# Subtractions from split operands joined in PSUM, and eight modulation slabs loaded ahead of the first x tiles, in a hybrid transformer block

## The chip, the cores and the metric

The kernel runs on one core of a Trainium2 chip. Time is device microseconds of one execution, lower is better. The kernel before took 1477.26, 1480.0 and 1477.43 us in three runs, median 1477.43.

## The reference

One block works on 1024 latent tokens and 256 context tokens of width 1024, in fp32. Cut to what matters here:

```python
mod = jax.nn.silu(c) @ lp['w_mod'] + lp['b_mod']      # w_mod is 1024 x 6144
sh1, sc1, g1, sh2, sc2, g2 = jnp.split(mod[:, None, :], 6, axis=-1)
h = _rms(x, lp['norm1']) * (1 + sc1) + sh1
P = _project(h, lp, rope)                              # one projection: Fourier, attention, delta rule
...
x = x + g1 * _mix_out(P, o_att, o_dn, lp['w_out'], lp['o_norm'])
x = x + g2 * _mlp(_rms(x, lp['norm2']) * (1 + sc2) + sh2, lp['w_ff1'], lp['w_ff2'])

def _mlp(h, w1, w2):
    u = jnp.maximum(h @ w1, 0.0)
    return (u * u) @ w2
```

The context tokens go through the same modulation (from c_ctx) and projection, and only feed the attention and the delta rule.

## The kernel before, in words

**Numbers in two halves.** A product in fp32 is made of three matmuls: each operand is held as a high part, rounded to the matmul's type fp32r, and a low part, the remainder. `mm3` (L238 to L241) issues high × high, high × low, low × high; so the lines L239, L240 and L241 are most of TensorE's rows. `split` (L1452 to L1454) makes the halves: ACT writes the high part (the line of the helper is L223), and an engine given by the caller subtracts it from the value to get the low part (L1454).

**Engines and queues.** V is VectorE (DVE in the profile), G is GpSimd (POOL), T is TensorE (PE), SC is ScalarE (ACT), Y is SyncE (SP), whose queue issues nearly all loads. A scheduler decides the order of each engine's instructions from the order of the code and priorities (`tc.high_priority`); where `ypin` or `pinned` is set, loads (`yd`, L231) or matmuls (`pe`, L229) keep the order of the code. Each engine works through its own queue in order.

**The start.** w_mod is read in slabs of 128 × 1024 (512 KB), eight slabs for each sixth of the modulation (a "pass", q). `mod_steps` (L314) loads one slab and issues four matmuls on it for each of its steps. Slabs live in a ring of eight buffers, later nine (L340, L406). The order of the code is: pass 0 interleaved with the transposes of the first two x tiles (L403 to L414), the columns of the modulation, pass 1 (L417), then the first projections. `load_x` (L361) loads x tiles, `rms_rows` (L354) squares and sums a tile on ACT and takes the power on POOL (L357, L358), `norm_in` (L367) scales it on DVE (L370). The rope tables are prepared on POOL at L389 to L398. The passes 4, 2 and 5 come later, as small tasks between other matmuls, from a ring of two slabs; their loads stand on SP's queue among writes to and reads from DRAM scratch (lsc, L710 and L723; tsc, L733; qd, L770).

**The MLP's operands.** The MLP multiplies by blocks, with seven products in place of eight, for which sums and differences of blocks are needed. The modulated h of the second norm is held transposed, in blocks of eight pieces of 128 × 512. `h2_first` makes the first half's blocks, named "11" and "21", as high and low parts in the dictionary HB. `h2_second` (L1539) makes the other operands:

- t1[k] = transposed second half, piece k, less block 11's piece k
- t2[k] = piece k + 4 (called 22) less t1[k]; 22[k] is that piece itself
- t3[k] = t2[k] less block 11's piece k; t4[k] = t2[k] less block 21's piece k

Only the parts of 11 and 21 exist, so a subtraction of one takes two steps: the high part (`sub` on G, or on V for k = 0), then the low part (on V), all at L1540. `h2_T` (L1446) transposes one piece: four transposes on PE (L244) into a bank of PSUM, then ACT scales it out to SBUF. Its banks come from the ring `tr2`, which holds three of the eight banks at that point: bk[0], bk[1], bk[3] (L1498).

`h2_second` is issued at high priority (L1618). Around it `ff1` (L1565) makes the products for the first two column blocks j = 0, 1: "11" and "12" first, then s1 (which uses t1), s2 (t2), s4 (22), s3 (t3) and 22 (t4), each evicted from PSUM by ACT or DVE (L1583 to L1613). `w1_prep` (L1481) makes the weights' side: sums on POOL (L1487), high parts on ACT, low parts on DVE (L1454). `gate_bc` (L1348) spreads a row of the modulation over all partitions: two small matmuls on PE (L236) and one DVE operation (L1352). In the profile a tile is named by its pool: fbase and z2a to z2c hold fp32, rbase, z1a to z1d hold fp32r, ba and bk are PSUM banks.

Of the kernel before, what the change touches and what calls it, by code (L numbers as in the profile page):

```python
# [14 lines left out]
ALU = mybir.AluOpType  # L15
AX = mybir.AxisListType

P = 128
D = 1024
# [3 lines left out]
KT = D // P  # L23
# [171 lines left out]
def body(tc, t, out):  # L195
# [3 lines left out]
    with ctx:  # L199
# [14 lines left out]
        V, G, T, Y, SC = nc.vector, nc.gpsimd, nc.tensor, nc.sync, nc.scalar  # L214

        def buf(*shape, top=False, a=None, at=None):
            return Buf(a or Fa, (P,) + shape, top, at)

        def rbuf(*shape, a=None):
            return Buf(a or Ra, (P,) + shape)  # L220
# [4 lines left out]
        def f32(ap):  # L225
            return ap.bitcast(F32)


        def pe(i):  # L229
            return tc.keep_in_program_order(i) if pinned else i  # L230

        def yd(i):
            return tc.keep_in_program_order(i) if ypin else i

        def mm(o, l, r, start, stop):
            pe(T.matmul(o, l, r, start=start, stop=stop))  # L236
# [15 lines left out]
        C = {k: cstb[a >= 256]()[:, a % 256 if a < 256 else a - 256 : b if a < 256 else b - 256] for k, (a, b) in CST.items()}  # L252
# [21 lines left out]
        cs = csb()  # L274
# [35 lines left out]
        def mod_pass(*a):  # L310
            for _ in mod_steps(*a):
                pass

        def mod_steps(q, slabs, bank, queue=Y):  # L314
            w = t["w_mod"]
            for k in range(KT):
                sl = slabs.next()
                sl = sl if isinstance(sl, tuple) else (sl,)
                n = D // len(sl)
                for z, part in enumerate(sl):  # L320
                    yd(queue.dma_start(part, w[0, k * P : (k + 1) * P, q * D + z * n : q * D + (z + 1) * n]))
                for g in range(4):
                    mm(bank[32 * g : 32 * g + 32, 0:256], cs[:, k, :], sl[g * 256 // n][:, g * 256 % n : g * 256 % n + 256], k == 0, k == KT - 1)
                yield

        def mod_cols(bank, sets, rowbuf):
# [11 lines left out]

        rowtmp = buf(256)
        slab0 = [buf(D, a=Z2) for _ in range(8)]  # L340
        slabs = Ring([b() for b in slab0])

# [24 lines left out]
        def norm_in(xs):  # L367
            for xt in xs:
                rs = rms_rows(xt)
                V.tensor_scalar(xt, xt, rs, None, op0=ALU.mult)  # L370
# [32 lines left out]
        ypin = True  # L403
        xs0 = load_x(t["x"][0], 0, xb[0:2])
        norm_in(xs0)
        slab1 = [buf(D, a=Z2)]  # L406
        xTb = [buf(256) for _ in range(KT)]
        trb = Ring([bk[0], bk[1]])
        slabs = Ring([b() for b in slab0 + slab1])
        for k, _ in enumerate(mod_steps(0, slabs, bk[2])):  # L410
            b = trb.next()
            for q, xt in enumerate(xs0):
                tp(b[:, q * P : (q + 1) * P], xt[:, k * P : (k + 1) * P])
            act(xTb[k](), b[:, 0:256])  # L414
# [72 lines left out]
        ypin = False  # L487
# [39 lines left out]
        for p, xs in enumerate((xs1, xs2, xs3, xs4)):  # L527
            norm_in(xs)
            g, c0 = ((0, 256), (1, 0), (1, 256), (2, 0))[p]
# [104 lines left out]
        b = gb.next()  # L634
# [9 lines left out]
        b = gb.next()  # L644
# [8 lines left out]
        b = gb.next()  # L653
# [5 lines left out]
        for d in range(2):  # L659
# [32 lines left out]
        sub = Arena(Z2.base, 0)  # L692
# [56 lines left out]
        def modulations():  # L749
            (v,) = mod_rows(bk[2], 1, rowtmp())  # L750
            V.tensor_tensor(kt2(s2()), v, kt2(col[:, r_b2 : r_b2 + 8]), op=ALU.add)
            yield
            yield from mod_steps(4, mslr, bk[2])
            act(rowtmp(), bk[2][:, 0:256])
            yield
            (v,) = mod_rows(bk[2], 1, rowtmp())
            V.tensor_tensor(kt2(a2()), v, kt2(col[:, r_b2 + 8 : r_b2 + 16]), op=ALU.add)
            V.scalar_tensor_tensor(a2(), a2(), 1.0, col[:, r_n2 : r_n2 + 8], op0=ALU.add, op1=ALU.mult)
            yield
            for q, z in ((2, 0), (5, 1)):  # L760
                yield from mod_steps(q, mslr, bk[2])
                act(mrowb[z](), bk[2][:, 0:256])
                yield
# [605 lines left out]
        for n in range(NPR * 5):  # L1369
            j, k = n // 5, n % 5  # L1370
# [59 lines left out]
        rw = [[buf(4, 256) for _ in range(2)], None]  # L1430
        shr = Ring([buf(512) for _ in range(3)])
        tr2 = Ring([bk[0], bk[1]])

        def rms_ff(q):
            st = rsb[q]()
            for z in range(2):
                act(bk[2], ACC[q][:, z * 512 : z * 512 + 512], AF.Square, accum_out=st[:, z : z + 1])
            G.tensor_tensor(st[:, 0:1], st[:, 0:1], st[:, 1:2], op=ALU.add)
            G.tensor_scalar(st[:, 0:1], st[:, 0:1], 1.0 / D, EPS, op0=ALU.mult, op1=ALU.add)
            G.tensor_tensor(st[:, 1:2], st[:, 0:1], neghalf[:, 0:1], op=ALU.pow)  # L1440
# [5 lines left out]
        def h2_T(k, hf):  # L1446
            b = tr2.next()
            for q in range(4):
                tp(b[:, q * P : (q + 1) * P], ACC[q][:, k * P : (k + 1) * P])
            act(hf, b, AF.Identity, scale=a2()[:, k : k + 1], bias=s2()[:, k : k + 1])  # L1450

        def split(i, hi, lo, eng, heng=None):  # L1452
            (heng or act)(hi, i)
            eng.tensor_tensor(lo, i, f32(hi), op=ALU.subtract)  # L1454
# [37 lines left out]
        for n4 in range(4):  # L1492
# [9 lines left out]
            for q in range(NT):  # L1502
                b = omr.next()[:, 0:256]
# [26 lines left out]
        HB = {"11": [tuple(x()[:, k] for x in B11) for k in range(4)], "21": [tuple(x()[:, k] for x in B21) for k in range(4)]}  # L1530
# [6 lines left out]
        ur = Ring(slot[14:16] + slot[0:8:2] + slot[1:8:2] + slot[8:14])  # L1537

        def h2_second():  # L1539
            sub = lambda e, o, i, x: e.tensor_tensor(o, i, x, op=ALU.subtract)  # L1540
            t1, tr_ = [x() for x in slot[8:12]], Ring([x() for x in slot[12:14]])
            for k in range(4):
                h2_T(k, t1[k])
                sub(G if k > 0 else V, t1[k], t1[k], f32(HB["11"][k][0]))
                sub(V, t1[k], t1[k], f32(HB["11"][k][1]))
                split(t1[k], *HB["t1"][k], V)
            for k in range(4):
                h22 = tr_.next()
                h2_T(k + 4, h22)
                sub(V, t1[k], h22, t1[k])  # L1550
                split(t1[k], *HB["t2"][k], V)
                split(h22, *HB["22"][k], V)
            for k in range(4):
                x3 = tr_.next()
                sub(G, x3, t1[k], f32(HB["11"][k][0]))
                sub(V, x3, x3, f32(HB["11"][k][1]))
                split(x3, *HB["t3"][k], G)
                sub(G, t1[k], t1[k], f32(HB["21"][k][0]))
                sub(V, t1[k], t1[k], f32(HB["21"][k][1]))
                split(t1[k], *HB["t4"][k], V)  # L1560

        f1r = Ring(A3 + bk[2:5])
# [55 lines left out]
        with tc.high_priority(OFN3):  # L1618
            h2_second()
# [33 lines left out]
        zp2, Z2 = zone("right", Z2W, F32, "z2c")  # L1653
# [69 lines left out]
        for pn, (prods, blocks) in enumerate(PASSES):  # L1723
            for pc in range(NPC):
# [4 lines left out]
                for w in blocks:  # L1729
                    W[w] = raww.next()()  # L1730
                    j, k = int(w[0]) - 1, int(w[1]) - 1
# [7 lines left out]
                if pn == 3 and pc in (2, 3, 4, 5):  # L1739
                    q = pc - 2  # L1740
                    gated(y11[q], q, 0, lo_h)
                    gated(m3[q], q, 0, hi_h)
                for n in prods:
                    if n in WSUM:
                        x, y, op = WSUM[n]
                        V.tensor_tensor(W[x], W[x], W[y], op=op)
                        w = W[x]
                    else:
                        w = W[WRAW[n]]
# [34 lines left out]
```

## Time and profile before

| | us |
|---|---|
| three runs: median (lowest, highest) | 1477.43 (1477.26, 1480.0) |
| the profiled execution | 1475.22 |
| its span, first to last instruction | 1473.1 |
| PE busy | 1391.9 |
| DVE busy | 1026.7 |
| ACT busy | 704.6 |
| POOL busy | 657.2 |

The profiled execution is 2.2 us shorter than the median of the three runs; the span lacks 2.1 us of it. Its granted clock of TensorE is 0.972 of full speed on average. A row of the timeline gives start and length in us, engine, line, operation, the tile written and the tiles read, partitions × elements, a count, and in brackets how long the engine was idle before it and which engine and line ended that. Rows of a matmul overlap the next one: the distance of two starts is the rate. A row with "x4" stands for four instructions in a row.

### The profile page before, as it was taken

The page shows a single profiled execution, that of the slowest core. Times are in us where ns is not written, and L with a number is a line of the kernel's source. Part 1 is how long each engine was busy: PE and PEld are TensorE (multiplying, and loading weights), DVE is VectorE, ACT ScalarE, POOL GpSimd, SP SyncE. Part 2 cuts the span into 40 slices and gives each one's busy share as a digit, 9 for nine tenths or more (in the row PEclk, how much of TensorE's full clock was granted, in tenths as well). Part 3 has the DMA queues.
Part 4 walks back from the last instruction along what each step waited for, and adds up shares of the span by engine and source line. Part 5 has one row for each costly group of instructions (what it writes and reads, how often), then busy time and mean ns, then how long its engine had stood idle before and what let it go on. Part 6 is the DMA issues. An engine that isn't in the chain of part 4 may idle for free.

```text
span 1473.1 us, 28890 instructions
## 1 busy us (share of the span) xinstructions
PE 1391.9 (94%) x11438; PEld 1118.6 (76%) x11438; DVE 1026.7 (70%) x1747; ACT 704.6 (48%) x1239; POOL 657.2 (45%) x698
## 2 busy tenths in 40 slices
PE   5899888989999999989899789999999999999998
PEld 1787866766777777768799667888888888888886
DVE  0876688775878777786733898755556677676884
ACT  1743312223777777776512645554555443443331
POOL 2764653632446466465433866444343100020782
PEclk8799999989999999999999889999999999999999
DMA  9414374552001010042222214544445898776641
GB/s 327 176 58 141 95 186 122 148 109 79 9 9 25 5 36 10 10 148 72 87 82 105 92 49 143 164 152 156 158 157 185 296 395 271 249 236 210 200 158 57
DMA packets 137302, 197.65 MB, mean 134 GB/s; under 512 B 45021, under 2 KB 80463, under 8 KB 136911
## 3 DMA queue, kind: packets, MB, share of 16 engines
q1 hardware_dynamic: 136464, 195.12, 41.2%
q8 instruction: 89, 1.46, 0.4%
q10 hardware_dynamic: 703, 0.69, 0.2%
q14 instruction: 46, 0.38, 0.1%
HBM read 149.84 MB, written 45.94 MB: 133 GB/s over the span
## 4 chain that ended last, share of the span: by engine, by line
PE 46%; DVE 5%; POOL 2%; issue 1%; DMA 1%; ACT 0%; DVEq 0%; POOLq 0%; ACTq 0%; SPq 0%
PE bk L240 8%; PE bk L241 8%; PE bk L239 8%; PE ba L239 7%; PE ba L240 7%; PE ba L241 7%; DVE fbase L1540 1%; PE bk L236 1%; DVE z1c L1454 1%; DVE z1b L1321 0%; DVE rbase L984 0%; DMA fbase<-la 0%; POOL rbase L1454 0%; PE ba L236 0%; POOL z2c L1714 0%
## 5 line engine op out<-in xcount | busy, mean ns | idle before, releaser
L223 ACT ACTIVATE rbase<-fbase 128x512 fp32r<-128x512 f32 (+3 forms) x255 | 171.9, 686 | 87.6 <-PE bk L240 55.3
L223 ACT ACTIVATE fbase<-bk 128x512 f32<-128x512 f32 (+3 forms) x224 | 124.9, 561 | 150.8 <-PE bk L236 93.8
L236 PE MATMUL bk<-rbase 128*128 128x256 f32 (+1 forms) x960 | 164.5, 307 | 2.1 <-DVE rbase L984 1.1
L236 PEld LDWEIGHTS bk<-rbase 128*128 128x128 f32 (+1 forms) x960 | 127.0, 173 | 30.4 <-DVE rbase L984 1.9
L236 PE MATMUL ba<-rbase 128*65 128x512 f32 (+4 forms) x576 | 137.7, 341 | 6.3 <-DVE rbase L984 4.6
L223 ACT ACTIVATE z1c<-fbase 128x512 fp32r<-128x512 f32 (+1 forms) x120 | 76.7, 654 | 135.3 <-DMA fbase<-w_ff 49.1
L223 ACT ACTIVATE fbase<-fbase 128x512 f32<-128x512 f32 (+4 forms) x148 | 95.8, 660 | 94.5 <-POOL fbase L1606 27.2
L1487 POOL TENSOR_TENSOR fbase<-fbase 128x512 f32<-128x512 f32 x64 | 89.2, 1395 | 110.7 <-DVE z1c L1454 101.5
L1688 POOL TENSOR_TENSOR z2c<-z2c,fbase 128x512 f32<-128x512 f32 x16 | 31.8, 2010 | 203.6 <-ACT z2c L223 128.6
L960 DVE TENSOR_REDUCE fbase<-ba 128x1 f32<-128x512 f32 (+1 forms) x192 | 106.4, 594 | 19.6 <-PE ba L236 18.2
L223 ACT ACTIVATE rbase<-z1d 128x1024 fp32r<-128x1024 f32 x61 | 63.1, 1055 | 101.2 <-PE bk L240 87.3
L1454 DVE TENSOR_TENSOR z1c<-fbase,z1c 128x512 fp32r<-128x512 f32 x112 | 96.3, 866 | 19.2 <-ACT z1c L223 15.8
L1454 DVE TENSOR_TENSOR rbase<-z1d,rbase 128x1024 fp32r<-128x1024 f32 x61 | 85.5, 1416 | 31.8 <-ACT rbase L223 31.7
L984 POOL TENSOR_TENSOR rbase<-fbase,rbase 128x512 fp32r<-128x512 f32 x56 | 72.1, 1288 | 67.2 <-ACT rbase L223 63.1
L239 PE MATMUL bk<-rbase 128*128 128x512 f32 x256 | 99.6, 389 | 0.0
L240 PE MATMUL bk<-rbase 128*128 128x512 f32 x256 | 99.6, 389 | 0.0
L241 PE MATMUL bk<-rbase 128*128 128x512 f32 x256 | 99.6, 389 | 0.0
L984 DVE TENSOR_TENSOR rbase<-fbase,rbase 128x512 fp32r<-128x512 f32 x104 | 81.0, 779 | 24.6 <-ACT rbase L223 23.9
L1454 DVE TENSOR_TENSOR rbase<-fbase,rbase 128x1024 fp32r<-128x1024 f32 (+1 forms) x63 | 79.7, 1285 | 22.6 <-ACT rbase L223 22.5
L236 PEld LDWEIGHTS ba<-rbase 128*65 128x65 f32 (+1 forms) x576 | 75.7, 154 | 23.9 <-DVE rbase L984 5.7
L240 PE MATMUL ba<-rbase 128*128 128x512 f32 x192 | 74.7, 389 | 0.0
L241 PE MATMUL ba<-rbase 128*128 128x512 f32 x192 | 74.7, 389 | 0.0
(346 smaller groups left out, 3842.6 us busy)
## 6 DMA issues: line engine op xcount, KB each, us to landing
fbase<-w_ff SPq DMA_DIRECT2D x70, 512.0 KB
u<-fbase SPq DMA_DIRECT2D x112, 256.0 KB
z1d<-w_ff SPq DMA_DIRECT2D x34, 512.0 KB
z1d<-u SPq DMA_DIRECT2D x33, 512.0 KB
fbase<-w_mod SPq DMA_DIRECT2D x32, 512.0 KB
fbase<-u SPq DMA_DIRECT2D x23, 512.0 KB
z2a<-w_mod SPq DMA_DIRECT2D x16, 512.0 KB
fbase<-w_in SPq DMA_DIRECT2D x16, 512.0 KB
```

The lines of the kernel that those rows point to most:

```text
L223: return SC.activation(o, i, f, **k)
L236: pe(T.matmul(o, l, r, start=start, stop=stop))
L239: pe(T.matmul(o, lh, rh, start=start, stop=False))
L240: pe(T.matmul(o, lh, rl, start=False, stop=False))
L241: pe(T.matmul(o, ll, rh, start=False, stop=stop))
L960: V.tensor_reduce(st4[:, z : z + 1], b, AX.X, ALU.max)
L984: (G if k2 in GP and not any(a <= n < b for a, b in NGP) else V).tensor_tensor(hl[:, :, 1], p, f32(hl[:, :, 0]), op=ALU.subtract)
L1454: eng.tensor_tensor(lo, i, f32(hi), op=ALU.subtract)
L1487: G.tensor_tensor(w[nm], w[a], w[b], op=op)
L1540: sub = lambda e, o, i, x: e.tensor_tensor(o, i, x, op=ALU.subtract)
L1688: G.tensor_tensor(c, c, G2[cs_.start // 512], op=ALU.mult)
```

## The change

It has two parts.

1. The eight slabs of pass 0 are loaded as soon as the ring is made, and the ring has nine buffers from the start. These loads are pinned, so they stand on SP's queue ahead of the x tiles. `mod_steps` takes a slab that is already there from the dictionary `early`. A branch for slabs in several parts, which is no longer used, is dropped.
2. In `h2_second`, `joined(nm, k)` adds the high and the low part of a piece in PSUM: two matmuls with an identity (`idb`, copied to fp32r once) into a bank of `tr2`. One DVE subtract with that bank as an operand replaces the two subtracts. The low part of t3 is made on V, not on G.

```diff
+        early = {}
+
+        def slab_load(q, k, slabs, queue=Y):
+            sl = slabs.next()
+            yd(queue.dma_start(sl, t["w_mod"][0, k * P : (k + 1) * P, q * D : (q + 1) * D]))
+            return sl
+
         def mod_steps(q, slabs, bank, queue=Y):
...
+                sl = slab_load(q, k, slabs, queue) if (q, k) not in early else early.pop((q, k))
                 for g in range(4):
...
         slab0 = [buf(D, a=Z2) for _ in range(8)]
-        slabs = Ring([b() for b in slab0])
+        slab1 = [buf(D, a=Z2)]
+        slabs = Ring([b() for b in slab0 + slab1])
+        ypin = True
+        for k in range(KT):
+            early[0, k] = slab_load(0, k, slabs)
+        ypin = False
...
+        idb = rbuf(P)
+        V.tensor_copy(idb(), C["ident"])
...
         def h2_second():
-            sub = lambda e, o, i, x: e.tensor_tensor(o, i, x, op=ALU.subtract)
+            sub = lambda o, i, x: V.tensor_tensor(o, i, x, op=ALU.subtract)
             t1, tr_ = [x() for x in slot[8:12]], Ring([x() for x in slot[12:14]])
+
+            def joined(nm, k):
+                b = tr2.next()
+                for z in range(2):
+                    mm(b, idb(), HB[nm][k][z], z == 0, z == 1)
+                return b
+
             for k in range(4):
                 h2_T(k, t1[k])
-                sub(G if k > 0 else V, t1[k], t1[k], f32(HB["11"][k][0]))
-                sub(V, t1[k], t1[k], f32(HB["11"][k][1]))
+                sub(t1[k], t1[k], joined("11", k))
                 split(t1[k], *HB["t1"][k], V)
...
             for k in range(4):
                 x3 = tr_.next()
-                sub(G, x3, t1[k], f32(HB["11"][k][0]))
-                sub(V, x3, x3, f32(HB["11"][k][1]))
-                split(x3, *HB["t3"][k], G)
-                sub(G, t1[k], t1[k], f32(HB["21"][k][0]))
-                sub(V, t1[k], t1[k], f32(HB["21"][k][1]))
+                sub(x3, t1[k], joined("11", k))
+                split(x3, *HB["t3"][k], V)
+                sub(t1[k], t1[k], joined("21", k))
                 split(t1[k], *HB["t4"][k], V)
```

The order of instructions differs from the start to about 215 us, and in the stage of `h2_second`; the rest is the same. PE has 24 matmuls more. POOL has 15 operations fewer (eleven subtracts and four low halves). DVE has one subtract fewer, four low halves and one small copy more. Line numbers after are those of the changed kernel: L318 is the slab's load, L371 the x tile's, L1547 the subtract, L1461 the low half, L236 on rbase 128x512 a join's matmul.

At the start SP's queue read, before:

```order
L364 DMA fbase<-x 128x1024 x2
L321 DMA z2a<-w_mod 128x1024 x12
L321 DMA fbase<-w_mod 128x1024
L321 DMA z2a<-w_mod 128x1024 x4
L439 DMA fbase<-w_in 128x4x256
```

and now:

```order
L318 DMA z2a<-w_mod 128x1024 x8
L371 DMA fbase<-x 128x1024 x2
L318 DMA z2a<-w_mod 128x1024 x7
L318 DMA fbase<-w_mod 128x1024
L318 DMA z2a<-w_mod 128x1024
L444 DMA fbase<-w_in 128x4x256
```

Eight slabs have passed the two x tiles; the single slab of a later pass (into fbase) has moved from the thirteenth to the sixteenth place among the slabs.

Further on, at about 240 us, the slabs of a later pass stand beside four writes to the scratch tsc. SP before:

```order
L321 DMA fbase<-w_mod 128x1024 x3
L733 DMA tsc_1282<-z2a 8x32x32 x4
L321 DMA fbase<-w_mod 128x1024
L723 DMA z2a<-lsc_1280 32x32x32
L881 DMA fbase<-tsc_1282 128x256
```

and now:

```order
L318 DMA fbase<-w_mod 128x1024 x4
L738 DMA tsc_1282<-z2a 8x32x32 x4
L318 DMA fbase<-w_mod 128x1024
L728 DMA z2a<-lsc_1280 32x32x32
L886 DMA fbase<-tsc_1282 128x256
```

One slab more is issued ahead of the four writes.

In `h2_second`, PE before, from the last product of "12" (bk_78) to the first ones with t1 (z2b, into bk_80); bk_76, bk_77 and bk_79 are the three banks of `tr2`:

```order
L241 MATMUL bk_78<-rbase,z1c 128x512
L244 MATMUL bk_79<-fbase 128x128 x4
L244 MATMUL bk_76<-fbase 128x128 x4
L244 MATMUL bk_77<-fbase 128x128 x4
L244 MATMUL bk_79<-fbase 128x128 x4
L239 MATMUL bk_80<-z2b,z1c 128x512
L244 MATMUL bk_76<-fbase 128x128 x4
L240 MATMUL bk_80<-z2b,z1c 128x512
```

and now:

```order
L241 MATMUL bk_78<-rbase,z1c 128x512
L236 MATMUL bk_79<-rbase 128x512 x2
L244 MATMUL bk_76<-fbase 128x128 x4
L236 MATMUL bk_77<-rbase 128x512 x2
L244 MATMUL bk_79<-fbase 128x128 x4
L239 MATMUL bk_80<-z2b,z1c 128x512
L240 MATMUL bk_80<-z2b,z1c 128x512
L241 MATMUL bk_80<-z2b,z1c 128x512
L236 MATMUL bk_76<-rbase 128x512 x2
L239 MATMUL bk_80<-z2b,z1c 128x512
L244 MATMUL bk_77<-fbase 128x128 x4
L240 MATMUL bk_80<-z2b,z1c 128x512
```

Joins (L236) alternate with transposes on the three banks, and products with t1 stand between them.

DVE at the same place, before:

```order
L1540 TENSOR_TENSOR fbase<-fbase,rbase 128x512 x2
L1454 TENSOR_TENSOR z1c<-fbase,z1c 128x512
L1540 TENSOR_TENSOR fbase<-fbase,rbase 128x512
L1591 TENSOR_TENSOR fbase<-bk_78,fbase 128x512
L1454 TENSOR_TENSOR z1c<-fbase,z1c 128x512
L1540 TENSOR_TENSOR fbase<-fbase,rbase 128x512
L1454 TENSOR_TENSOR z2b<-fbase,z2b 128x512
```

and now:

```order
L1547 TENSOR_TENSOR fbase<-fbase,bk_76 128x512
L1547 TENSOR_TENSOR fbase<-fbase,bk_79 128x512
L1461 TENSOR_TENSOR z1c<-fbase,z1c 128x512
L1461 TENSOR_TENSOR z2b<-fbase,z2b 128x512
L1461 TENSOR_TENSOR z1c<-fbase,z1c 128x512
L1547 TENSOR_TENSOR fbase<-fbase,bk_77 128x512
L1461 TENSOR_TENSOR z2b<-fbase,z2b 128x512
```

Each subtract reads a bank, and the low halves of t1 (into z2b) stand closer behind them.

More of the change, by code (lines that the diff above doesn't have):

```diff
@@ L312, in mod_pass @@
                 pass
+        early = {}
[3 more added lines that the diff above has]
+            return sl
         def mod_steps(q, slabs, bank, queue=Y):
-            w = t["w_mod"]
             for k in range(KT):
[L317 to L321, printed above, removed]
+                sl = slab_load(q, k, slabs, queue) if (q, k) not in early else early.pop((q, k))
                 for g in range(4):
-                    mm(bank[32 * g : 32 * g + 32, 0:256], cs[:, k, :], sl[g * 256 // n][:, g * 256 % n : g * 256 % n + 256], k == 0, k == KT - 1)
+                    mm(bank[32 * g : 32 * g + 32, 0:256], cs[:, k, :], sl[:, g * 256 : g * 256 + 256], k == 0, k == KT - 1)
                 yield
@@ L405, in body @@
         norm_in(xs0)
-        slab1 = [buf(D, a=Z2)]
         xTb = [buf(256) for _ in range(KT)]
         trb = Ring([bk[0], bk[1]])
-        slabs = Ring([b() for b in slab0 + slab1])
         for k, _ in enumerate(mod_steps(0, slabs, bk[2])):
@@ L1549, in h2_second @@
                 h2_T(k + 4, h22)
-                sub(V, t1[k], h22, t1[k])
+                sub(t1[k], h22, t1[k])
                 split(t1[k], *HB["t2"][k], V)
```

## The prediction

> **What bounds the kernel now.** I read the page first, the busy totals and the chain that ended last:
>
> ```profile
> span 1473.1 us, 28890 instructions
> PE 1391.9 (94%) x11438; PEld 1118.6 (76%) x11438; DVE 1026.7 (70%) x1747; ACT 704.6 (48%) x1239; POOL 657.2 (45%) x698
> PE 46%; DVE 5%; POOL 2%; issue 1%; DMA 1%; ACT 0%; DVEq 0%; POOLq 0%; ACTq 0%; SPq 0%
> ```
>
> TensorE (PE) is the bound over most of the span, so a change gains only where PE idles or runs slowly. Both edits touch such places. The windows (span, then busy time of PE, PEld, DVE, ACT, POOL, granted clock, DMA share, GB/s) show them beside a full one:
>
> ```profile
> 0.00:37.00 37.00, 19.39 (x150) 6.38 (x150) 3.01 (x12) 7.54 (x17) 9.24 (x23) 0.88 0.92 328
> 814.00:851.00 37.00, 26.95 (x144) 20.81 (x142) 33.99 (x37) 23.70 (x45) 29.96 (x26) 0.81 0.27 90
> 851.00:888.00 37.00, 35.45 (x125) 25.27 (x126) 35.11 (x38) 17.11 (x30) 29.01 (x17) 0.87 0.12 36
> 925.00:962.00 37.00, 37.00 (x161) 29.96 (x160) 26.17 (x35) 18.76 (x34) 16.57 (x12) 1.00 0.55 183
> ```
>
> From 0 to 37 us the DMA engines are 92% busy: the load bounds. From 814 to 888 DVE is 93% busy, POOL 80%, DMA idle, and PE is short of work. This is h2_second, where the operands t1, t2, 22, t3, t4 of the MLP are made. PE's own rows there (start, length, line, and in brackets the idle time before and what ended it):
>
> ```profile
> 836.29 1.70 PE L244 MATMUL bk<-fbase 128*128 128x128 f32 x8 [1.66 <-ACT fbase L223]
> 848.45 0.80 PE L240 MATMUL bk<-z2b,z1c 128*128 128x512 f32 x1 [4.86 <-DVE z2b L1454]
> 849.04 0.63 PE L241 MATMUL bk<-z2b,z1c 128*128 128x512 f32 x1
> 849.47 0.63 PE L239 MATMUL bk<-z2b,z1c 128*128 128x512 f32 x1
> 851.05 0.80 PE L240 MATMUL bk<-z2b,z1c 128*128 128x512 f32 x1 [0.95 <-DVE z2b L1454]
> ...
> 859.55 0.39 PE L241 MATMUL bk<-z2b,z1c 128*128 128x512 f32 x1
> 859.77 0.39 PE L239 MATMUL bk<-z2b,z1c 128*128 128x512 f32 x1
> ...
> 875.85 0.69 PE L236 MATMUL bk<-fbase 1*128 1x256 f32 x2 [0.94 <-DVE fbase L1352]
> 879.49 0.79 PE L239 MATMUL ba<-rbase,z1c 128*128 128x512 f32 x1 [0.56 <-DVE fbase L1602]
> 880.09 0.63 PE L240 MATMUL ba<-rbase,z1c 128*128 128x512 f32 x1
> 880.51 0.63 PE L241 MATMUL ba<-rbase,z1c 128*128 128x512 f32 x1
> ...
> 889.55 0.39 PE L239 MATMUL ba<-z2b,z1c 128*128 128x512 f32 x1
> ```
>
> PE waits for DVE to finish t1's low halves (z2b, L1454). Its matmuls start 0.23 us apart at 859.6, but 0.43 apart at 849 and 880, right behind the gaps: the granted clock is half there. So an idle microsecond costs again afterwards.
>
> Why DVE is late shows in its rows and POOL's:
>
> ```profile
> 842.69 1.75 DVE L1540 TENSOR_TENSOR fbase<-fbase,rbase 128x512 f32<-128x512 f32 x1
> 846.05 1.75 DVE L1540 TENSOR_TENSOR fbase<-fbase,rbase 128x512 f32<-128x512 f32 x1
> 848.50 0.69 DVE L1540 TENSOR_TENSOR fbase<-fbase 128x512 f32<-128x512 f32 x1
> 873.68 0.68 DVE L1598 TENSOR_TENSOR fbase<-ba,fbase 128x512 f32<-128x512 f32 x1
> 842.18 1.72 POOL L1540 TENSOR_TENSOR fbase<-fbase,rbase 128x512 f32<-128x512 f32 x1
> 873.17 1.74 POOL L1540 TENSOR_TENSOR fbase<-fbase,rbase 128x512 f32<-128x512 f32 x1
> L1540 DVE TENSOR_TENSOR fbase<-fbase,rbase x13: 684/1766/1775, 837.7 to 885.5; 128x512 f32<-128x512 f32 x13
> L1540 POOL TENSOR_TENSOR fbase<-fbase,rbase x11: 1292/1733/2883, 838.8 to 879.9; 128x512 f32<-128x512 f32 x11
> ```
>
> A subtract of two SBUF tiles takes 0.69 us on DVE while POOL rests (848.50) and 1.75 while POOL computes (842.69 beside 842.18): the two engines take turns. With one operand in PSUM (ba, at 873.68, POOL busy from 873.17) it takes 0.68 all the same.
>
> **The change, part by part.**
>
> *Joins.* Per element before: one POOL subtract and one DVE subtract, in series (k=0 of t1: both on DVE). After: two 128x512 matmuls on PE into a PSUM bank, one DVE subtract from it. Removed: 12 subtracts of the high parts (11 POOL, 1 DVE) and 12 DVE subtracts of the low parts, median 1.77. Added: 24 matmuls on PE and 12 DVE subtracts with a PSUM operand, taken at 0.68 from the row at 873.68. Four low-half splits move from POOL to DVE, at 0.69 (like 848.50, POOL now idle) to 1.77. So on DVE: 12 × (1.77 − 0.68) = 13 off, 4 × 0.69 = 2.8 on, one subtract off; POOL loses 15 operations of about 1.7, and DVE's other operations no longer take turns with these. DVE's 51 us (837.7 to 889) come to some 36 to 40. What POOL keeps, the sums of w1 and two of L1600's kind, still costs about a microsecond of DVE each.
>
> What this is worth on PE. I walked the new order by hand, each DVE operation started 0.6 us after the one before or when its input is there. The last low half of t1 ends near 847.6, where PE's row at 851.05 waits now: 4 us earlier, less 0.5 for starting the walk's joins in the same in-order queue. PE then has, counted in its order, the remaining 111 matmuls × 0.233 = 25.9, sixteen join matmuls × 0.233 = 3.7, four pairs of gate matmuls at 0.62 to 0.69 (875.85), 2.5, and one half-clock stretch as at 849, 2.5: 34.6, to about 882. Before, the same point is reached at 889.5 (the row at 889.55). So **−7.5 us**. In other words: 4 from t1, about 3.5 plus 4 from the second half of the stage (t3 and t4 ready near 867 instead of 888, so that the gaps of 875.85 and 879.49 and their half clock fall away), less 3.7 for joins that lie on PE's path. The first eight join matmuls lie in the gaps before 848.
>
> Bounds. Below: everything lost goes. In the two windows from 814 to 888 PE idles 74 − 26.95 − 35.45 = 11.6, and the clock withheld costs about 0.19 × 26.95 + 0.13 × 35.45 = 9.7: 21 in all. Some 3 of it lie ahead of t1's first transposes at 836, and joins take back 3.7 to 5.6: at best −14. Above: t1 comes no earlier and only the second half gains what the joins cost: −1. The row of 7.52 below is the one that draws me to the middle: POOL starts t3 only when t2 is split (9.85 idle), then DVE waits for it, and both go.
>
> ```profile
> 857.10 7.52 POOL L1540 TENSOR_TENSOR fbase<-fbase,rbase 128x512 f32<-128x512 f32 x4 [9.85 <-DVE rbase L1454]
> 860.02 3.46 DVE L1540 TENSOR_TENSOR fbase<-fbase,rbase 128x512 f32<-128x512 f32 x2 [1.19 <-POOL fbase L1540]
> ```
>
> A new wait: a join takes a bank of the three that the transposes also use. A transpose for k+2 stands in PE's queue behind a bank that DVE's subtract must first empty, and products of t1 stand behind it. That is in the walk; its failure is a rival.
>
> A page of the Trainium skill speaks against this. "TensorE: Matmul & The Clock Gate", section "A second HAM failure mode: psum-queue depth-cycling", says that PE, cycling through PSUM banks, idles for moments between groups often enough that its clock keeps falling back. This trace has half clock behind a gap of 4.86 us and again after 875; whether short gaps alone do it no run here shows. It is the third rival.
>
> The identity copy is one small DVE cast: nothing.
>
> *Early loads.* The queue now issues eight slabs, the two x tiles, then the other slabs; the bytes ahead of the last slab are the same. PE's rows at the end of this load:
>
> ```profile
> 33.66 0.64 PE L236 MATMUL bk<-z2a,fbase 128*32 128x256 f32 x8 [0.65 <-DMA z2a<-w_mod]
> 34.97 1.08 PE L236 MATMUL bk<-z2a,fbase 128*32 128x256 f32 x8 [0.67 <-DMA z2a<-w_mod]
> 38.52 0.82 PE L239 MATMUL ba<-z1a,rbase 128*128 128x272 f32 x2 [1.22 <-ACT rbase L223]
> ```
>
> Slabs land 1.3 us apart and PE waits for each, so the last lands when it did and no gain follows. What moves is x: its tiles land some eight slabs (10 us) later, and their norm now stands on POOL behind the first six of eight rope products:
>
> ```profile
> 14.85 0.55 POOL L358 TENSOR_TENSOR fbase<-fbase 128x1 f32<-128x1 f32 x1
> 16.91 0.75 DVE L370 TENSOR_SCALAR fbase<-fbase 128x1024 f32<-128x1024 f32 x1 [0.59 <-POOL fbase L358]
> 22.25 2.77 POOL L398 TENSOR_TENSOR fbase<-fbase 128x256 f32<-128x256 f32 x4
> ```
>
> The products end near 25; 0.55 + 0.75 for each of two tiles makes x ready at 27.6 instead of 17.7. PE then has 16 transposes and six slabs, 6.5 to 10.6 us by its clock: done at 34.2 to 38.2, where 36.05 is the end of the slab row at 34.97. I take **+0.5**, with 0 to +2.
>
> *Other slabs.* The ring of w_mod slabs shifts by one in SP's in-order queue further on. Of PE's waits for them:
>
> ```profile
> 193.75 1.08 PE L236 MATMUL bk<-fbase 128*32 128x256 f32 x8 [4.54 <-DMA fbase<-w_mod]
> 246.46 0.64 PE L236 MATMUL bk<-fbase 128*32 128x256 f32 x8 [1.78 <-DMA fbase<-w_mod]
> 250.31 0.64 PE L236 MATMUL bk<-fbase 128*32 128x256 f32 x8 [0.92 <-DMA fbase<-w_mod]
> 240.31 2.10 SPq L733 DMA_DIRECT2D tsc<-z2a x4
> 242.52 0.43 SPq L321 DMA_DIRECT2D fbase<-w_mod x1
> ```
>
> The slab issued at 242.52 stood behind four writes of tsc, 2.1 us long; now it is ahead of them. PE's 1.78 goes and most of 0.92 stays or goes: **−1.5**, 0 to −2.7. The slab waited for at 193.75 goes the other way, behind one more write of lsc: **+0.5**, −0.5 to +1.5.
>
> Sum: −7.5 + 0.5 − 1.5 + 0.5 = **−8.0**. The profiled execution took 1475.22 (span 1473.1 and 2.1 around it); it becomes 1467.2. The median of the three runs, 1477.43, lies 2.2 above the profiled one, so I forecast **1469.4**, its own range 1464 to 1474.4.
>
> **The rivals.**
>
> *The whole loss goes* (−14): t1 comes by 845, the joins hide, no half clock. For it: DVE alone feeds the stage and loses all turn-taking. Against: the ramp still needs DVE operation after operation. 1475.22 − 14 − 0.5 + 2.2: 1463.
>
> *Nothing gained* in h2_second: DVE's taking of turns was not what ended last; PE's gap at 836.29 waits for ACT, not DVE, and ACT's share stays as it is. Then t1 moves by a microsecond, the joins take it back: −1 − 0.5 + 2.2 on 1475.22: about 1476.
>
> *The clock falls back between joins.* In rows: a stretch like 849 to 854 or 880 to 885 loses 2.5 us; three more of them cancel 7.5. 1477. The skill's section named above gives this way.
>
> *Slower*: the three banks. If a subtract holds its bank for the 1.2 us that a DVE operation and its queue take before the next transposes can be written, eight times in a row before t2 is complete, t1's four arrive as late as before, and all 24 join matmuls land on PE's path, 24 × 0.233 = 5.6, at half clock partly more. It decides once the banks' turn exceeds the 3.4 us that t1's elements are apart today (DVE at 842.69 and 846.05). 1477.43 + 5.6 − 1.0: 1482.
>
> **How the numbers follow.** Forecast 0.58, whole loss 0.18, nothing gained 0.10, clock 0.06, slower 0.08. A difference under 0.2%, 3 us, cannot be told from none, so faster is below 1474.5 and slower above 1480.4. Faster: 0.56 + 0.18 + 0.04 = 0.78. Same: 0.02 + 0.06 + 0.05 = 0.13. Slower: 0.01 + 0.08 = 0.09. The range holds the forecast, most of the whole loss and half of nothing gained: 1461.5 to 1476.5.
>
> **What would show it.** Right: DVE's subtracts of L1547 at 0.68 throughout; PE's wait of 4.86 at 848 shortened to about 1; POOL nearly empty from 846 to 872; a full PE by 882 and the rest of the trace as it was, about 8 earlier; the wait of 1.78 at 246 gone. Wrong: a subtract with its PSUM operand over 1 us; a wait of PE for L1547 in front of transposes; half clock from 850 to 880; first projection later than 40 us.

## The result, and the profile after

The changed kernel takes 1467.45 us (median of four runs, 1466.84 to 1467.98); the kernel before took 1478.38 in the same comparison (four runs, 1477.26 to 1480.0). The ratio is 0.9925, with a 95% interval from 0.9908 to 0.9942: 11 us faster. The forecast was 1469.4, with 1461.5 to 1476.5 as its range.

The page of the changed kernel, its size, busy totals and chain:

```profile
span 1466.0 us, 28924 instructions
PE 1389.7 (95%) x11462; PEld 1119.7 (76%) x11462; DVE 1014.2 (69%) x1751; ACT 704.5 (48%) x1239; POOL 630.8 (43%) x683
PE 49%; DVE 2%; POOL 2%; ACT 1%; issue 1%; DVEq 0%; POOLq 0%; ACTq 0%
```

The span is 7.1 us shorter and the share of DVE in the chain has gone from 5% to 2%. The four windows:

```profile
0.00:37.00 37.00, 18.39 (x140) 5.67 (x140) 3.10 (x12) 6.93 (x15) 9.28 (x23) 0.89 0.88 315
814.00:851.00 37.00, 32.48 (x176) 26.59 (x173) 33.48 (x42) 25.86 (x48) 25.57 (x24) 0.91 0.29 97
851.00:888.00 37.00, 36.43 (x153) 27.73 (x152) 32.14 (x47) 19.97 (x35) 13.87 (x9) 1.00 0.22 72
925.00:962.00 37.00, 37.00 (x162) 29.90 (x161) 24.41 (x35) 20.54 (x36) 17.08 (x14) 1.00 0.49 160
```

In h2_second PE runs 176 and 153 records where it ran 144 and 125, at a granted clock of 0.91 and 1.00 in place of 0.81 and 0.87. POOL falls to 13.87 in the second window. The first window has got worse: 315 GB/s in place of 328.

PE's rows in the stage:

```profile
836.88 0.73 PE L236 MATMUL bk<-rbase 128*128 128x512 f32 x2 [1.75 <-ACT fbase L223]
839.00 1.11 PE L244 MATMUL bk<-fbase 128*128 128x128 f32 x4 [1.39 <-DVE fbase L1547]
839.77 1.20 PE L236 MATMUL bk<-rbase 128*128 128x512 f32 x2
...
842.05 0.63 PE L240 MATMUL bk<-z2b,z1c 128*128 128x512 f32 x1
...
846.57 0.66 PE L244 MATMUL bk<-fbase 128*128 128x128 f32 x4 [0.48 <-DVE fbase L1547]
...
848.67 0.39 PE L239 MATMUL bk<-z2b,z1c 128*128 128x512 f32 x1
848.90 0.39 PE L239 MATMUL ba<-rbase,z1c 128*128 128x512 f32 x1
...
864.57 0.47 PE L239 MATMUL ba<-z2b,z1c 128*128 128x512 f32 x1 [0.57 <-DVE fbase L1609]
```

The wait of 4.86 us for t1's low half is gone. What is left is the wait for ACT (1.75), two waits of transposes for a bank that a subtract has yet to empty (1.39 and 0.48), and 0.57 later on. Windows that follow the granted clock (it stands ahead of the last two numbers), first of the kernel before:

```profile
834.00:837.00 3.00, 1.33 (x8) 0.65 (x6) 3.00 (x4) 2.27 (x5) 2.31 (x2) 1.00 0.00 0
837.50:854.00 16.50, 8.94 (x26) 5.72 (x25) 16.36 (x19) 12.49 (x22) 9.74 (x6) 0.50 0.30 95
854.50:857.00 2.50, 2.50 (x13) 2.00 (x12) 2.50 (x6) 2.04 (x4) 0.00 (x0) 1.00 0.01 3
```

and of the changed kernel:

```profile
838.50:844.50 6.00, 5.50 (x18) 4.27 (x19) 5.96 (x7) 5.89 (x12) 4.40 (x3) 0.50 0.44 132
845.00:857.00 12.00, 11.52 (x57) 9.29 (x56) 11.34 (x20) 10.15 (x18) 0.00 (x0) 1.00 0.17 61
```

The first stretch at half clock (a granted clock of 0.50) lasts 6.8 us in place of 17.1 (read from windows of half a microsecond), and a second one, from 878 to 885 before, is gone. DVE and POOL in the changed kernel:

```profile
838.27 1.27 DVE L1547 TENSOR_TENSOR fbase<-fbase,bk 128x512 f32<-128x512 f32 x2
843.45 0.67 DVE L1547 TENSOR_TENSOR fbase<-fbase,bk 128x512 f32<-128x512 f32 x1
848.25 0.68 DVE L1461 TENSOR_TENSOR z2b<-fbase,z2b 128x512 fp32r<-128x512 f32 x1
870.37 0.69 DVE L1461 TENSOR_TENSOR z1c<-fbase,z2b 128x512 fp32r<-128x512 f32 x1
836.20 6.78 POOL L1494 TENSOR_TENSOR fbase<-fbase 128x512 f32<-128x512 f32 x4 [0.70 <-DVE z1c L1461]
864.57 1.62 POOL L1611 TENSOR_TENSOR fbase<-fbase 128x512 f32<-128x512 f32 x1 [21.59 <-DVE fbase L1609]
```

A subtract from PSUM takes 0.67, also at 838.27, while POOL computes. The last low half of t1 ends at 848.9 (851.6 before), the last of t4, the row at 870.37, at 871.1 (889.0 before). POOL rests for 21.59 us.

At the start, PE's last rows of the slabs and the first projection:

```profile
34.85 0.64 PE L236 MATMUL bk<-z2a,fbase 128*32 128x256 f32 x8 [1.40 <-DMA z2a<-w_mod]
35.42 0.44 PE L244 MATMUL bk<-fbase 128*128 128x128 f32 x2
37.48 1.08 PE L236 MATMUL bk<-z2a,fbase 128*32 128x256 f32 x8 [1.62 <-DMA z2a<-w_mod]
...
40.98 0.82 PE L239 MATMUL ba<-z1a,rbase 128*128 128x272 f32 x2 [1.22 <-ACT rbase L223]
```

The last slab lands 2.5 us later than before, and so the projections begin 2.5 later.

**A measure for the stage.** Runs of one kernel differ by several us (the kernel before: 1472.5 to 1483.6 in 23, 18 and 29 runs). To see the stage alone, I take the time from a pair of DVE's low halves that opens it, a row that all kernels have, to the end of the span. Before and after:

```profile
833.63 2.43 DVE L1454 TENSOR_TENSOR z1c<-fbase,z1c 128x512 fp32r<-128x512 f32 x2 [1.23 <-ACT z1c L223]
```

```profile
834.23 2.42 DVE L1461 TENSOR_TENSOR z1c<-fbase,z1c 128x512 fp32r<-128x512 f32 x2 [1.23 <-ACT z1c L223]
```

That is 1473.1 − 833.63 = 639.5 before and 1466.0 − 834.23 = 631.8 after: the stage gained 7.7 us. Ahead of it the changed kernel is 0.6 us late.

The windows of these two stretches have PE busy for 620.7 us before and 620.3 after. So PE's idle time there falls from 18.8 to 11.5 us, which is nearly all of the gain. Its busy time hardly changes: the 24 matmuls more, 24 × 0.233 = 5.6 us, are about made up for by the shorter half clock.

### The profile page after: what moved, and what is told of

It is laid out like the page before. It is cut to its first block, busy times and chain, and to the rows that moved or that the text cites. A ratio compares the mean times of both kernels' runs of the same rounds, so it can differ in the third digit from the quotient of the medians.

```text
span 1466.0 us, 28924 instructions
## 1 busy us (share of the span) xinstructions
PE 1389.7 (95%) x11462; PEld 1119.7 (76%) x11462; DVE 1014.2 (69%) x1751; ACT 704.5 (48%) x1239; POOL 630.8 (43%) x683
## 4 chain that ended last, share of the span: by engine, by line
PE 49%; DVE 2%; POOL 2%; ACT 1%; issue 1%; DVEq 0%; POOLq 0%; ACTq 0%
PE bk L240 8%; PE bk L241 8%; PE bk L239 8%; PE ba L239 8%; PE ba L240 8%; PE ba L241 8%; PE bk L236 2%; DVE z1b L1326 0%; PE ba L236 0%; POOL rbase L1461 0%; ACT fbase L223 0%; DVE rbase L989 0%; POOL z2c L1727 0%; POOL z2c L1725 0%; POOL z2b L1289 0%
## 5 line engine op out<-in xcount | busy, mean ns | idle before, releaser
L236 PE MATMUL bk<-rbase 128*128 128x256 f32 (+2 forms) x984 | 173.5, 311 | 3.9 <-ACT fbase L223 2.6
L236 PEld LDWEIGHTS bk<-rbase 128*128 128x128 f32 (+1 forms) x984 | 132.4, 175 | 33.7 <-ACT fbase L223 3.4
L236 PE MATMUL ba<-rbase 128*65 128x512 f32 (+4 forms) x576 | 138.4, 342 | 6.2 <-DVE rbase L989 4.8
L1461 DVE TENSOR_TENSOR z1c<-fbase,z1c 128x512 fp32r<-128x512 f32 x112 | 92.2, 826 | 23.9 <-ACT z1c L223 20.1
L1461 DVE TENSOR_TENSOR rbase<-z1d,rbase 128x1024 fp32r<-128x1024 f32 x61 | 85.1, 1411 | 27.3 <-ACT rbase L223 27.1
L1461 DVE TENSOR_TENSOR rbase<-fbase,rbase 128x1024 fp32r<-128x1024 f32 (+1 forms) x65 | 81.4, 1271 | 21.0 <-ACT rbase L223 20.7
L236 PEld LDWEIGHTS ba<-rbase 128*65 128x65 f32 (+1 forms) x576 | 76.2, 155 | 24.0 <-DVE rbase L989 5.9
```

## The experiments

Each kernel was timed against the kernel before, with an interval for the ratio; "stage" is the measure above, from one profile each. "First" is the start of the first projection.

| kernel | ratio (95%) | stage | first |
|---|---|---|---|
| before | 1 | 639.5 | 38.5 |
| changed | 0.9925 (0.9908 to 0.9942) | 631.8 | 41.0 |
| joins_only | 0.9948 (0.9931 to 0.9966) | 631.8 | 38.7 |
| early_only | 0.9991 (0.9978 to 1.0004) | 640.4 | 40.0 |
| all_dve | 0.9980 (0.9966 to 0.9994) | 638.0 | 39.2 |
| joins_t3pool | 0.9933 (0.9918 to 0.9949) | 631.7 | 37.9 |
| joins_t1 | 0.9963 (0.9949 to 0.9977) | 635.8 | 38.0 |
| joins_t34 | 0.9981 (0.9970 to 0.9992) | 638.3 | 38.6 |
| joins_two_banks | 0.9940 (0.9922 to 0.9957) | 632.8 | 38.7 |
| joins_double | 0.9955 (0.9937 to 0.9973) | 634.6 | 38.2 |
| joins_dve_more | 0.9992 (0.9978 to 1.0005) | 639.0 | 39.6 |
| joins_pool_more | 0.9977 (0.9965 to 0.9988) | 636.8 | 39.3 |
| after_t3pool | 0.9936 (0.9917 to 0.9955) | 632.1 | 39.8 |
| early_four | 0.9998 (0.9984 to 1.0012) | 640.4 | 40.0 |

Four kernels with all joins and no added work, the changed one among them, have a stage between 631.7 and 632.1, so a difference of 1 us from these can be told. The three with the old `h2_second` (before, early_only, early_four) lie between 639.5 and 640.4, so a gain against before is uncertain by about 1 us.

**Each part alone.** joins_only is the kernel before with `idb`, `joined` and the new `h2_second`; early_only is the changed kernel with the old `h2_second`.

> The kernel before with the joins in PSUM and nothing else: no early loads. Theory (the two parts add up, and h2_second carries the gain): between the profiles of before and after, the stage from 833 us on gained 7.7, while the start lost 2.5 and the stretch from 41 to 302 won 2.8. So joins alone: about -7.7 us, ratio 0.9948 (0.993 to 0.9965), the first projection back at 38.5 us and the slab waits of PE as before, 9 us in all. Rival (the early loads have a share of their own in the 10.9 us between the medians): -4 to -6 us, ratio 0.996 to 0.9975.

> The kernel before with the early loads and nothing else. Theory: 2.5 us lost at the start (first projection near 41.0) and 2.8 won until 302 us: -0.5 us, ratio 1.000 (0.9985 to 1.001). Rival (a share of its own in the gain): -3 us, ratio 0.998 or less. A third way, that only the loss at the start lasts: +2.5 us, ratio 1.0017.

The joins bring 7.7 us of the stage and 0.52% of the time; the early loads alone cannot be told from nothing. The theory held. early_only's stage is 1 us longer than before's, and so is early_four's; I have no reason for that.

**POOL's share without joins.** all_dve:

```diff
-                sub(G if k > 0 else V, t1[k], t1[k], f32(HB["11"][k][0]))
+                sub(V, t1[k], t1[k], f32(HB["11"][k][0]))
...
-                sub(G, x3, t1[k], f32(HB["11"][k][0]))
+                sub(V, x3, t1[k], f32(HB["11"][k][0]))
...
-                split(x3, *HB["t3"][k], G)
-                sub(G, t1[k], t1[k], f32(HB["21"][k][0]))
+                split(x3, *HB["t3"][k], V)
+                sub(V, t1[k], t1[k], f32(HB["21"][k][0]))
```

> The kernel before, with all subtracts and splits of h2_second on DVE and none on POOL: no joins, no early loads. DVE has 15 operations more than before, and 12 more than with joins. Theory (what hurt was the taking of turns of DVE and POOL; the joins only save DVE 12 operations of 0.6 us): every subtract takes 0.69, t1's last low half comes 2.4 us later than with joins and t4's 7 us later, still 15 us ahead of before; PE is spared 3.7 us of joins. -5 to -8 us, ratio 0.9945 to 0.9965. Rival (the one subtract in place of two is what counts, POOL's hands were worth their turns): between -2 and +2 us, ratio 0.9985 to 1.0015.

The stage gained 1.4 us only: the rival was nearer, though the ratio lies in neither range. Here, taking POOL out paid little with its work landing on DVE. PE's waits in the stage of all_dve and of joins_only (in total, times, longest):

```profile
PE bk L240 <- DVE z2b L1454: 5.0, 2, 4.2
PE bk L244 <- ACT fbase L223: 4.2, 3, 2.1
PE ba L240 <- DVE z2b L1454: 2.5, 2, 1.8
PE bk L244 <- DVE fbase L1444: 0.9, 1, 0.9
```

```profile
PE bk L244 <- DVE fbase L1542: 1.9, 2, 1.4
PE bk L236 <- ACT fbase L223: 1.7, 1, 1.7
PE bk L244 <- DVE fbase L1446: 0.9, 1, 0.9
PE ba L239 <- DVE fbase L1604: 0.6, 1, 0.6
```

With all on DVE, PE still waits for low halves (z2b), 4.2 us at the same place and later again. The order that the scheduler made of it differs too: it put five subtracts of t1 in a row. So this run alone does not show that DVE's load is the reason.

joins_t3pool left t3's low half on POOL, `split(x3, *HB["t3"][k], G)`.

> Joins alone, but the four low halves of t3 stay on POOL. Theory: POOL takes turns with DVE again at four places, 1.1 us of DVE each, between 855 and 870 us, where PE has work in store; against joins alone 0 to +1 us, ratio to before 0.995 (0.9935 to 0.997). Rival (DVE paces PE there too): +3 us or more against joins alone, ratio 0.997 or more.

Where PE has work in store, POOL's hand in it makes no difference: 631.7 against 631.8.

**The two halves.** joins_t1 joins only for t1, joins_t34 only for t3 and t4; the other subtracts are the old pairs.

> Only the four joins of t1; t3 and t4 as before (POOL and DVE, two subtracts each). Start as before. Theory of the prediction: t1's half brings some 3.5 to 4 us and its eight matmuls lie in gaps of PE: -3.5 us, ratio 0.9977 (0.9965 to 0.999). Rival (t1 only moves the wait to t3 and t4, which end at the same time as before): 0 to -1 us, ratio 0.9993 or more.

> Only the eight joins of t3 and t4; t1 as before. Theory of the prediction: the gaps at 876 and 879 us and their half clock go, and the sixteen matmuls cost 3.7 us of PE: -3.8 us, ratio 0.9974 (0.996 to 0.999). If the two halves add up, the ratios of this run and of the run with t1's joins multiply to 0.9948. Rival (all of the gain comes from t1, since PE has work in store after 858): +1 to +3 us, ratio 1.0005 to 1.002.

In the stage they gain 3.7 and 1.2, together 4.9 where both give 7.7. The product of the ratios, 0.9944, is close to 0.9948, so the timed runs would allow that the halves simply add up; the profiles speak against it. In them each alone meets the other's wait. PE's rows in joins_t1 that waited later:

```profile
868.85 1.21 PE L236 MATMUL bk<-fbase 1*128 1x256 f32 x2 [4.35 <-DVE fbase L1352]
870.89 0.77 PE L239 MATMUL ba<-z2b,z1c 128*128 128x512 f32 x1 [0.83 <-DVE fbase L1607]
```

PE comes to the gate's matmuls early and waits 4.35 us for DVE, which is at the old pairs of t3 and t4. In joins_t34 the 4.86 of t1 is as before. So t1's half starts the gain, and t3's and t4's half keeps it. The granted clock shows the same: joins_t1 has 3.4 us at half clock early in the stage and 6.8 later on, joins_t34 the 17.1 of before early and nothing later.

**Banks and matmuls.** joins_two_banks sets `tr2.items = [bk[0], bk[1]]` in `h2_second`; joins_double gives each join four matmuls:

```diff
-                for z in range(2):
-                    mm(b, idb(), HB[nm][k][z], z == 0, z == 1)
+                for z in range(4):
+                    mm(b, idb() if z < 2 else zdb(), HB[nm][k][z % 2], z == 0, z == 3)
```

> Joins alone, with two banks in place of three for transposes and joins in h2_second. In the profile of after PE waits 1.9 us in all for a subtract to empty a bank. Theory (banks cost little): 2 to 4 us over joins alone, ratio to before 0.9965 to 0.9975. Rival of the prediction (the banks decide): the ramp to t1 takes 4 to 8 us more and the gain is gone, ratio 0.9985 or more.

> Joins alone, with four matmuls in each join in place of two; the two more multiply by a block of zeros, so the sums are the same. Theory: of 24 more matmuls the eight of t1 lie in PE's gaps and sixteen cost 0.233 each: 3.7 us over joins alone, up to 5.6 if all lie on the path; ratio to before 0.9973 (0.9965 to 0.9985). Rival (PE has slack in the stage, joins are free): 0 to 1 us over joins alone, ratio 0.9948 to 0.9955.

Two banks cost 1.0 us of the stage, less than either side expected: the banks don't decide. (Its ratio, 0.9940, is no worse than that of joins_only.) 24 more matmuls cost 2.8 us of the stage. They are 24 × 0.233 = 5.6 us of work, but PE's busy time grows by 4.5 us only (624.8 against 620.3), since the half clock lasts 3.4 us in place of 6.8, and its idle time falls by 1.7 us (9.8 against 11.5).

**What paces the stage.** joins_dve_more and joins_pool_more add subtracts that nothing needs, on DVE and on POOL. joins_dve_more has `more(V, ...)` behind each subtract (twice for t4), joins_pool_more has `more(G, ...)` behind the splits:

```diff
+            spare = rbuf(384, a=Z1)()
+            more = lambda e, x, y: e.tensor_tensor(spare, x[:, 0:384], f32(y)[:, 0:384], op=ALU.subtract)
```

> Joins alone, with DVE work added that nothing needs: after each subtract a subtract of 384 columns into a spare tile (two for t4), 16 in all, as much as twelve of 512. It is about what DVE has to do in the run with all on DVE. Measured from the pair of low halves that opens the stage on DVE (833.63 us in the profile of before) to the end of the span: before 639.5, all on DVE 638.0, joins alone 631.8. Theory (DVE's time paces the stage, and the joins gain by halving its subtracts): 636 to 638, ratio to before 0.997 to 0.9985. Rival (two subtracts in a row, each waiting for the one before, are what counts, not DVE's time): below 634, ratio 0.995 to 0.9965.

> Joins alone, with POOL work added that nothing needs: a subtract of 384 columns of two SBUF tiles beside t1, t3 and t4, 15 in all, as much as the eleven subtracts of 512 that POOL had before. DVE's subtracts read PSUM, its splits read two SBUF tiles. Prediction's theory (the taking of turns made DVE late): +4 us or more on joins alone, stage to end 636 or more, ratio 0.9975 or more. New theory (turns cost little once the subtracts are halved and read PSUM): 0 to +2 us, stage to end 632 to 634, ratio 0.995 to 0.9965.

Both cost much: 7.2 us and 5.0 us of the stage. The first says that DVE's time paces the stage, beyond what I expected: PE idles 4.2 us more than in joins_only, 2.0 of them in a wait for DVE at 900, and has 13.6 us at half clock in place of 6.8. The second refutes my "new theory" and bears out the prediction's: work on POOL that nothing needs costs 4.9 us of PE's idle time. Most of this I put down to the taking of turns; POOL's own sums for the weights' side also come later in this run, and what that costs was not told apart. The DVE rows of joins_pool_more, and one of POOL, show the turns:

```profile
846.26 0.67 DVE L1542 TENSOR_TENSOR fbase<-fbase,bk 128x512 f32<-128x512 f32 x1
847.46 2.10 DVE L1542 TENSOR_TENSOR fbase<-fbase 128x512 f32<-128x512 f32 x2
858.65 1.51 DVE L1456 TENSOR_TENSOR z2b<-fbase,z2b 128x512 fp32r<-128x512 f32 x1
864.49 1.49 DVE L1456 TENSOR_TENSOR z2b<-fbase,z2b 128x512 fp32r<-128x512 f32 x1
867.10 1.87 DVE L1542 TENSOR_TENSOR fbase<-fbase,bk 128x512 f32<-128x512 f32 x3
870.69 2.50 DVE L1456 TENSOR_TENSOR z2b<-fbase,z2b 128x512 fp32r<-128x512 f32 x2
870.21 3.84 POOL L1544 TENSOR_TENSOR z1c<-z2b,rbase 128x384 fp32r<-128x384 f32 x3 [0.61 <-ACT z2b L223]
```

The subtracts from PSUM keep 0.67 (three in 1.87); the splits of two SBUF tiles grow from 0.68 to 1.5. This fits all_dve's small gain too: it removed most of the turns and put as much plain work in their place. The joins do both: they halve the number of subtracts, and so keep POOL's share of the work off DVE, and they end most of the turns.

**Variants.** after_t3pool is the changed kernel with t3's low halves on POOL; early_four is early_only with four slabs ahead of x in place of eight.

> The changed kernel, with the four low halves of t3 left on POOL. On joins alone this moved the stage by 0.1 us (631.8 to 631.7). Theory: nothing against the changed kernel, ratio to before 0.9925 to 0.994. Rival (POOL's help is worth something): 2 us better, 0.991 to 0.992.

> No joins; four slabs instead of eight are loaded ahead of the x tiles. With eight ahead, the loads' rate falls to a fifth near 17 us, and the first projection starts at 40.0 to 41.0 us in place of 37.9 to 39.2. Theory (the x tiles at that place of the queue, as the twelfth and thirteenth load, are what is held up): the dip is as before and the first projection starts at 38 to 39 us; the whole time within 2 us of before, ratio 0.9985 to 1.0015. Rival (any slabs ahead of x cost this, by the late norm of x): 39.5 to 41 us.

after_t3pool is no better than the changed kernel. early_four speaks for the rival at the start: with four slabs ahead the first projection is late as well, 40.0 in its one profile, where kernels without early loads have up to 39.6. But the rival's reason does not hold there. In early_four the squares of x run from 14.27 (13.34 before, 23.23 in the changed kernel), and PE at the end waits for the slab, as it does in the changed kernel:

```profile
33.81 0.64 PE L236 MATMUL bk<-z2a,fbase 128*32 128x256 f32 x8 [2.30 <-DMA z2a<-w_mod]
36.40 1.08 PE L236 MATMUL bk<-z2a,fbase 128*32 128x256 f32 x8 [0.58 <-DMA z2a<-w_mod]
```

No variant is better than the changed kernel by more than the intervals allow.

## Why the prediction was right, point by point

- **The stage, −7.5: right, 7.7 measured.** t1's half, 3.5 to 4: right, 3.7 alone. The second half, 3.5 plus 4 less 3.7 for joins: 1.2 alone, 4.0 on top of t1's. The sum holds because both are made; I had not said that the halves need each other. The joins were priced at 3.7; the nearest measurement, 24 more matmuls in joins_double, cost 2.8, so the price may be somewhat too high. "t3 and t4 ready near 867 instead of 888" was some 4 us too early: the last low half ends at 871.1 instead of 889.0.
- **Its reason: right, and incomplete.** POOL's work, and with it the turns, costs 5.0 us when put back. But ending the turns was only one half. The other is that POOL's subtracts did not come to DVE: DVE has only three operations more in the stage than before, where all_dve has fifteen more; a load like those twelve costs 7.2 us when put back. The two costs overlap and do not add up to the gain. all_dve, which ends most turns without saving the operations, gains 1.4.
- **The price of a subtract from PSUM, 0.68: right.** Twelve at 0.672 to 0.686, with POOL busy or not.
- **The three banks: seen, not decisive.** PE waited 1.39 and 0.48 for them, which the prediction had named as a sign of being wrong; it was in the walk all the same. A ring of two costs 1.0 more. The rival "slower" is out.
- **The clock falling back between joins: one stretch, as in the sum; but I had misread where it comes from.** I took the half clock of before at 849 to follow from the gap of 4.86 us. The windows above have it from 837.5 at the latest, 6 us before that gap began at 843.6, behind an idle time of 1.66 (the row at 836.29), and the second stretch, from 878, stands behind one of 0.94 (875.85). So the trace of before already showed what I said no run showed: half clock behind short gaps alone. PE was busy for 15.8 of its 23.9 us at half clock, and for 6.0 of 6.8 after, so at half speed PE lost 7.9 us before and 3.0 after. My sum had this gain only in part. What the rival needed, three stretches more, did not come: there is none after 845, with idle times of 0.48 and 0.57 left. So the rule of the Trainium skill that I weighed ("TensorE: Matmul & The Clock Gate", section "A second HAM failure mode: psum-queue depth-cycling") agrees with the trace in that the clock falls behind short idle times, here once; that it keeps falling back does not show here.
- **Early loads, +0.5 with 0 to +2: the size too small, and mostly by another way.** The profile has +2.5, and "first projection later than 40 us" was a sign of being wrong. Over the profiles, ten kernels without early loads start the projection between 37.9 and 39.6 (mean 38.7), four with them between 39.8 and 41.0 (mean 40.2): 1.5 us. I had blamed the late norm of x; DVE finished that at 28.7, near the 27.6 forecast, and in this profile PE was done with the transposes in time (35.42). The step that failed is that "the bytes ahead of the last slab are the same", from which I took that "the last lands when it did": its matmuls start at 37.48 in place of 34.97. SP's queue shows a hole:

```profile
1.90 11.96 SPq L318 DMA_DIRECT2D z2a<-w_mod x8
14.80 2.04 SPq L371 DMA_DIRECT2D fbase<-x x2
16.88 6.72 SPq L318 DMA_DIRECT2D z2a<-w_mod x7
```

  Between 13.86 and 16.88 it issues only the two x loads. From 16 to 20 us the DMA engines moved 179 GB/s, before 300; but joins_only, which has no early loads, has 227 there. So why the slab is late stays open, and early_four's lateness suggests that eight slabs ahead are not needed for it. In after_t3pool, with the same start, the blame on x holds after all: PE waits 2.04 us for the norm of x (at 29.62) and then runs through to the last slab without a wait for one:

```profile
29.62 0.69 PE L244 MATMUL bk<-fbase 128*128 128x128 f32 x2 [2.04 <-DVE fbase L377]
36.96 0.64 PE L236 MATMUL bk<-z2a,fbase 128*32 128x256 f32 x8
```

  So both ways occur, and which of them ends last differs between profiles.
- **Other slabs, −1.0: the parts partly wrong, the sum not to be told.** The wait at 246 went, but PE waited 1.98 for the next slab (at 248.22). The wait at 193 shrank to 2.92 where I had it grow. And then 1.7 us was lost again at a slab near 302 us. PE's wait there, before and after:

```profile
302.30 1.08 PE L236 MATMUL bk<-fbase 128*32 128x256 f32 x8 [6.74 <-DMA fbase<-w_mod]
```

```profile
301.92 1.08 PE L236 MATMUL bk<-fbase 128*32 128x256 f32 x8 [8.47 <-DMA fbase<-w_mod]
```

  The three kernels with eight early slabs wait 8.0 to 8.6 us here, the others 5.2 to 6.9: PE comes sooner and the slab does not. This slab's matmuls start at 301.8 us in the mean of the three and at 301.9 in the mean of the ten without early loads. So what the early loads lose or win ahead of 302 us is largely evened out, which fits early_only's 0.9991. I had seen this wait in the trace of before and left it out as unchanged. That the slab's arrival is what evens it out is read from the profiles, not tested.
- **"DMA idle" in the stage: loosely read.** The two windows have the DMA engines 0.27 and 0.12 busy; nothing in the sum rests on it.
- **Against the median: partly luck.** From profile to profile I forecast −8.0, and it came to −7.4. I added 2.2 us, by which the profile of before lay under its runs. The changed kernel's profile lies 0.4 above its median, and together 2.6, more than the 2 us by which the forecast was high. That the medians differ by 10.9 may owe something to the four runs of before: in the three later comparisons its median over 18 to 29 runs is 1476.65 to 1477.06. The parts measured alone, 0.9948 × 0.9991 = 0.9939, and after_t3pool, 0.9936, point to some 9 us.

## What to carry to other kernels

Where DVE paces a stage, count what it must do in that stage and what slows each operation: here the sum in PSUM took away half of the subtracts and most of the taking of turns with POOL, for 24 matmuls (24 more of them cost 2.8 us). Look, too, at the granted clock in fine windows: part of what a shorter wait is worth is the stretch at half clock that goes with it. Moving POOL's work to DVE, or leaving either load on, gave most of the gain back. An edit ahead of a load that arrives late anyway may be worth only what is left after it; look for that wait before costing the edit.

## What the runs showed of the hardware that I had not expected

- DVE's subtract with one operand in PSUM keeps 0.67 to 0.69 us beside a POOL operation on two SBUF tiles, while DVE operations on two SBUF tiles go from 0.68 to 1.5 and more (joins_pool_more; up to 1.78 in before). In this stage an operand in PSUM was a way past the turns.
- The time ahead of the slab near 302 us differs by 6 us between profiles (298.7 in joins_double, 304.5 in all_dve), though the kernels do the same there. Some 3 us of this is PE's waits for slabs of w_mod (25.5 and 28.9 us in all); the rest I have not traced. The stage from 833 us on repeats within 0.4 us in four kernels with the same joins, and within 1 us in three without.
- Half clock followed idle times of PE as short as 1.66 us (before, ending at 836.29), 1.75 us (changed kernel, 836.88) and 0.94 us (before, 875.85). In the fourteen profiles, between 820 and 930 us, every stretch at half clock lasted 3.4, 6.8, 10.2 or 17.1 us, by windows of half a microsecond: multiples of 3.4 us. So the stage's time has a grain: one such step more or less costs PE, as an estimate, up to half of 3.4 us.
